# First norm's sums from the feature-major input, the residual loaded later, features in 4 KB rows, the second chunk parted in halves

## The chip, the cores and the metric

The kernel runs on one core of a Trainium2 chip. The metric is the device time of one execution in microseconds; lower is better.

## What is computed

A segment of a decoder trunk on 256 tokens of width 2048, in f32: a recurrent layer (HGRN2) and then a differential-attention layer, each with an MLP and a gated embedding behind it. Only the beginning matters here: a norm over the features, and the projections that read it.

```
def rms_norm(x, gain):
    xf = x.astype(jnp.float32)
    y = xf * lax.rsqrt(jnp.mean(xf * xf, axis=-1, keepdims=True) + EPS)
    return (y * gain.astype(jnp.float32)).astype(x.dtype)
...
        h = rms_norm(x, ln_mix[i])
        if i < N_A:
            proj = h @ a_w_in[j]
            q_a, f_a, in_a, g_a = (t.reshape(b, s, A_HEADS, A_HEAD_DIM) for t in jnp.split(proj, 4, axis=-1))
            f = lb + (1.0 - lb) * jax.nn.sigmoid(f_a.astype(jnp.float32))
            o = hgrn2_chunkwise(jax.nn.silu(q_a), 1.0 - f, in_a, jnp.log(f))
            ...
            x = x + o.reshape(b, s, A_WIDTH).astype(x.dtype) @ a_w_out[j]
```

## The kernel before

All weights are read once, in chunks of 256 rows by 512 columns (512 KB each; `raw`, four buffers). A matrix product in nearly full f32 is made of parts: ACT rounds a chunk to a short format (`hi`, a cast), DVE subtracts that from the chunk (`lo`), and PE multiplies hi and lo with the activations, which are parted in the same way. hi and lo have three buffers each. A group is 512 output columns, eight chunks. In the groups used at the start (`group_b`: queries and forget gates, tokens as columns) each chunk gives PE eight pairs of matmuls, one hi 128x512 and one lo 128x256, into two PSUM tiles.

The gain of a norm is applied to its input ahead of the product (`gained`: one ACT instruction and one DVE instruction for each 128 features, here `gain_xa`), and the factor of each token, 1/sqrt(mean square), only to the result. So the first projection can start on x before its norm is known. x comes twice: `x_t` (features in partitions, 16 blocks of 128x256) into `xa`, two blocks a load, and `x_r` (tokens in partitions) into `x`, the residual, 512 columns a load. The first group is number 4, the first forget gates; group 0, the first queries, follows. `do_f` and `do_q` put the results through `project`, whose `evac` adds the halves of a PSUM tile and multiplies by the factor of the token, `RR[0]` (a row, the same in all partitions; `RR[1]` holds it with tokens in partitions).

Work that runs beside the chunks is written as generators (`gens`); `pump()` takes one step of each behind every chunk. `start()` is such a generator: per step it loads the next two blocks of `xa`, applies the gain, from the fifth step on loads a quarter of `x` and lets ACT square and sum it (`Norm.square`), and at the end DVE adds the sums, ACT takes the root (`rsqrt`: Ln and Exp), and a matmul of ones with a diagonal spreads the factors over all partitions. The compiler's scheduler then orders each engine's instructions; every engine runs its own in that order. All loads leave SP's queue in the order that it shows.

`accd` and the masks are POOL's only work; `lambdas()` and `bounds()` are small computations from the table `sml`. `x` is first used as the residual long after the start, where the layer's output is added. The chunks of a group are counted from 0 here, and "chunk 7" is the last one of group 4 where no group is named.

Of the kernel before, what the change touches and what calls it, by code (L numbers as in the profile page):

```python
# [17 lines left out]
P = 128  # L18
T = 256
# [20 lines left out]
def kernel(ctx: ExitStack, tc: tile.TileContext, a):  # L40
# [54 lines left out]
    def chunk(src):  # L95
        raw = rp.tile([P, KCS, CW], F32, tag="raw", name="raw")
        nc.sync.dma_start(raw.rearrange("p a b -> p (a b)"), src)
        hi = wp.tile([P, KCS, CW], F32R, tag="hi", name="hi")
        lo = wp.tile([P, KCS, CW], F32R, tag="lo", name="lo")
        nc.scalar.copy(hi, raw)  # L100
        nc.vector.tensor_tensor(lo, raw, hi.bitcast(F32), ALU.subtract)  # L101
        return hi, lo
# [48 lines left out]
    def group_b(wsrc, g, rhs, evac, pump=None, fresh=0, by_part=False):  # L151

        ps = [mm.tile([P, 2, CW], F32, tag="mm", name="mmps") for _ in range(2)]
        w = []
        for c in range(NCH):
            w.append((chunk if c or not fresh else first_chunk)(wsrc[g, c]))
            if c < fresh:
                mm_first(ps, *w[c], rhs, c)  # L160
            else:
                mm_b(ps[0], *w[c], rhs, 0, c * KCS, c == 0, c == NCH - 1, by_part and c == 0)
                for d in ([c] if fresh or c > 1 else [0, 1] if c else []):
                    mm_b(ps[1], *w[d], rhs, 1, d * KCS, d == 0, d == NCH - 1)
            if pump:
                pump()
        for pair in range(2):
            evac(4 * (g % 4) + 2 * pair, ps[pair])
# [36 lines left out]
    class Norm:  # L205
        def __init__(self, outs=(), row=False):
            self.outs, self.row = outs, row
# [27 lines left out]
        def finish(self, box):  # L235
# [4 lines left out]
            if self.row:  # L240
                dg = ev.tile([P, T], F32, tag="rr", name="dg", bufs=1)
                for tt in range(2):
                    nc.vector.tensor_scalar(dg[:, tt * P:(tt + 1) * P], ident, rc[:, tt, 0:1], None, ALU.mult)
                ps = sm.tile([P, 512], F32, tag="sm", name="smps")
                nc.tensor.matmul(ps[:, :T], ones, dg, start=True, stop=True)
                r = ev.tile([P, T], F32, tag="rn", name="rn", bufs=2)
                nc.scalar.copy(r, ps[:, :T])
            else:
                r = ev.tile([P, 2, 1], F32, tag="r2", name="r2", bufs=2)
                nc.vector.tensor_tensor(r, rc, rc, ALU.mult)  # L250
# [72 lines left out]
    nrm = Norm(row=True)  # L323
# [7 lines left out]
    def load_xa(c):  # L331
        nc.sync.dma_start(xa[:, 2 * c:2 * c + 2], a["x_t"][:, 2 * c:2 * c + 2])
# [45 lines left out]

    def start():

        for c in range(8):
            if c < 7:
                load_xa(c + 1)
                gain_xa(c + 1)
            if c == 3:
                nc.sync.dma_start(sml, a["small"])
                nc.sync.dma_start(ident, a["ident"])
            if c == 6:
                bounds()
            if c > 3:  # L390
                g = c - 4
                nc.sync.dma_start(x[:, :, g * CW:(g + 1) * CW], a["x_r"][:, :, g * CW:(g + 1) * CW])
                nrm.square(g)
            if c < 7:
                yield
        yield from nrm.finish(RR)
        for _ in range(4):
            yield
        for b in range(2):
# [3 lines left out]
        lambdas()  # L403

# [3 lines left out]
    with hs:  # L408
# [134 lines left out]
        def project(g):  # L543
# [3 lines left out]
            def evac(m, ps):  # L547
# [5 lines left out]
                nc.vector.tensor_tensor(t, lo, t, ALU.add)  # L553
                nc.vector.tensor_tensor(o, t, bc(RR[0], 2).rearrange("p m (c t) -> p m c t", c=2), ALU.mult)
# [4 lines left out]
        def do_f(j):  # L559
            s = st[j]  # L560
            z = project(4 + j)
# [369 lines left out]
```

## Time and profile before

| | us |
|---|---|
| median of 3 runs (lowest, highest) | 2508.78 (2508.29, 2509.92) |
| the profiled execution | 2508.73 |
| its span in the trace | 2506.9 |
| PE busy | 2497.7 |
| DVE busy | 1544.4 |
| ACT busy | 1301.8 |
| POOL busy | 7.1 |

The span runs from the first to the last instruction of the trace; the execution's own time holds some 2 us around it. PE is busy nearly all the time by the profile, so its idle stretches are few, and they are found in the waits of PE, in the chain of waits that ended last, and by reading the timeline. "PEld" is the load of weights into PE, which runs beside the matmuls. An f32 matmul is two instructions in the profile where its operands are not of the rounded kind.

### The profile page before, as it was taken

Reading aid. Unit: us, or ns where it says so; the run is one execution under the profiler, and the core shown is the slowest. Engines: PE = TensorE matmul, PEld = TensorE weight load, DVE = VectorE, ACT = ScalarE, POOL = GpSimd, SP = SyncE. Lnnn points to the kernel's source line nnn. Section 1 sums busy time; section 2 is a strip of 40 time slices with the busy share of each in tenths; the row PEclk is TensorE's granted clock in tenths of the full one; section 3 lists DMA queues with packets and bytes.
Section 4 is the critical chain, followed back from the end, with each engine's and each line's share of the span. In section 5 each row is a group of like instructions: output and inputs, shape, how many; then the busy total and the mean of one; then the engine's idle time right before and its main releaser. Section 6 shows DMA issues by size and latency. Waiting matters only on the chain.

```text
span 2506.9 us, 32220 instructions
## 1 busy us (share of the span) xinstructions
PE 2497.7 (100%) x12546; PEld 2113.1 (84%) x12546; DVE 1544.4 (62%) x1755; ACT 1301.8 (52%) x1659; POOL 7.1 (0%) x12
## 2 busy tenths in 40 slices
PE   9999999999999999999999999999999999999999
PEld 8888888888888888888888888888888888888887
DVE  7887886555565465565575576556555556555555
ACT  8666665544344444444576565544434434444455
POOL 0000000000000000000000000000000000000000
PEclk9999999999999999999999999999999999999999
DMA  7545455555555555565555545555556555555555
GB/s 274 181 152 180 160 169 180 185 188 191 193 190 195 193 187 193 193 192 186 187 180 188 185 151 173 167 184 187 193 187 194 192 193 190 196 190 189 189 188 168
DMA packets 130377, 466.99 MB, mean 186 GB/s; under 512 B 14512, under 2 KB 14896, under 8 KB 130224
## 3 DMA queue, kind: packets, MB, share of 16 engines
q1 hardware_dynamic: 130080, 464.93, 56.3%
q8 instruction: 98, 1.61, 0.3%
q14 instruction: 55, 0.45, 0.1%
q10 hardware_dynamic: 144, 0.01, 0.0%
HBM read 462.78 MB, written 2.10 MB: 185 GB/s over the span
## 4 chain that ended last, share of the span: by engine, by line
PE 96%; DVE 2%; ACT 1%; DMA 1%; issue 1%; SPq 0%; DVEq 0%; ACTq 0%
PE mmps L145 23%; PE mmps L178 19%; PE mmps L176 19%; PE mmps L177 19%; PE mmps L148 11%; PE smps L225 1%; PE smps L487 1%; DVE lo L101 1%; DMA x<-x_r 0%; PE smps L754 0%; PE smps L817 0%; PE smps L789 0%; DMA raw<-w_in 0%; ACT hi L100 0%; PE smps L518 0%
## 5 line engine op out<-in xcount | busy, mean ns | idle before, releaser
L101 DVE TENSOR_TENSOR lo<-raw,hi 128x1024 fp32r<-128x1024 f32 x871 | 1065.2, 1224 | 877.9 <-ACT hi L100 877.2
L100 ACT CAST hi<-raw 128x1024 fp32r<-128x1024 f32 x871 | 914.8, 1051 | 1052.8 <-PE mmps L178 618.8
L145 PE MATMUL mmps<-big,hi 128*128 128x512 f32 x2544 | 885.9, 394 | 0.0
L176 PE MATMUL mmps<-hi,big 128*128 128x512 f32 x2176 | 853.8, 392 | 0.0
L178 PE MATMUL mmps<-hi,big 128*128 128x512 f32 x2176 | 848.2, 390 | 0.0
L177 PE MATMUL mmps<-lo,big 128*128 128x512 f32 x2176 | 848.1, 390 | 0.0
L148 PE MATMUL mmps<-big,lo 128*128 128x256 f32 x2544 | 704.3, 278 | 0.3 <-DVE lo L101 0.3
L145 PEld LDWEIGHTS mmps<-big,hi 128*128 128x128 f32 x2544 | 476.3, 188 | 108.4
L178 PEld LDWEIGHTS mmps<-hi,big 128*128 128x128 f32 x2176 | 408.5, 188 | 85.9 <-DVE big L123 0.3
L148 PEld LDWEIGHTS mmps<-big,lo 128*128 128x128 f32 x2544 | 478.3, 188 | 2.8 <-DVE lo L101 0.9
L177 PEld LDWEIGHTS mmps<-lo,big 128*128 128x128 f32 x2176 | 408.8, 188 | 82.4
L176 PEld LDWEIGHTS mmps<-hi,big 128*128 128x128 f32 x2176 | 408.7, 188 | 82.1
L303 DVE SCALAR_TENSOR_TENSOR x<-mmps,r,x 128x512 f32<-128x512 f32 x64 | 45.1, 747 | 13.1 <-PE mmps L178 13.1
L201 ACT ACTIVATE big<-smps,sml 128x256 fp32r<-128x256 f32 x96 | 41.1, 471 | 18.1 <-DVE big L202 18.1
L123 DVE TENSOR_TENSOR big<-u,big 128x512 fp32r<-128x512 f32 x72 | 49.4, 686 | 0.0
L202 DVE SCALAR_TENSOR_TENSOR big<-smps,sml,big 128x256 fp32r<-128x256 f32 x96 | 42.3, 479 | 6.8 <-ACT big L201 6.5
L636 DVE SCALAR_TENSOR_TENSOR u<-u 128x512 f32<-128x512 f32 x64 | 44.3, 692 | 2.2
L122 ACT CAST big<-u 128x512 fp32r<-128x512 f32 x72 | 44.4, 616 | 1.9 <-DVE u L636 1.9
L294 ACT COPY t<-mmps 128x512 f32<-128x512 f32 x64 | 37.3, 583 | 14.5 <-PE mmps L148 14.5
L295 DVE TENSOR_TENSOR u<-mmps,t 128x512 f32<-128x512 f32 x64 | 43.8, 684 | 0.0
L213 ACT ACTIVATE t<-x 128x512 f32<-128x512 f32 x48 | 30.2, 630 | 3.8 <-DVE x L666 2.5
L487 PEld LDWEIGHTS smps<-B,A 128*128 128x128 f32 x160 | 20.0, 191 | 2.7 <-DVE on L528 1.1
(193 smaller groups left out, 892.8 us busy)
## 6 DMA issues: line engine op xcount, KB each, us to landing
raw<-w_up SPq DMA_DIRECT2D x256, 512.0 KB, 3.9
raw<-w_dn SPq DMA_DIRECT2D x256, 512.0 KB, 3.3
raw<-w_in SPq DMA_DIRECT2D x127, 512.0 KB, 3.3
raw<-w_pg SPq DMA_DIRECT2D x64, 512.0 KB, 3.3
raw<-w_ao SPq DMA_DIRECT2D x32, 512.0 KB, 3.3
raw<-w_k SPq DMA_DIRECT2D x32, 512.0 KB, 3.7
raw<-w_q SPq DMA_DIRECT2D x32, 512.0 KB, 3.9
raw<-w_v SPq DMA_DIRECT2D x32, 512.0 KB, 3.3
```

The source lines that it names most:

```text
L100: nc.scalar.copy(hi, raw)
L101: nc.vector.tensor_tensor(lo, raw, hi.bitcast(F32), ALU.subtract)
L122: nc.scalar.copy(dst[:, k, 0, :], src)
L123: nc.vector.tensor_tensor(dst[:, k, 1, :], src, dst[:, k, 0, :].bitcast(F32), ALU.subtract)
L145: nc.tensor.matmul(ps[:, ml, :], hi[:, k, w:w + P], rhs[:, k0 + k].rearrange("p a t -> p (a t)"), start=first and k == 0, stop=False)
L148: nc.tensor.matmul(ps[:, ml, T:2 * T], lo[:, k, w:w + P], rhs[:, k0 + k, 0, :], start=False, stop=last and k == KCS - 1)
L176: nc.tensor.matmul(out, xs[:, kc0 + k, 0, ts], hi[:, k], start=st, stop=False)
L177: nc.tensor.matmul(out, xs[:, kc0 + k, 0, ts], lo[:, k], start=False, stop=False)
L178: nc.tensor.matmul(out, xs[:, kc0 + k, 1, ts], hi[:, k], start=False, stop=en)
L303: nc.vector.scalar_tensor_tensor(xg, ps[:, tt], scale[:, tt, 0:1], xg, ALU.mult, ALU.add)
L487: nc.tensor.matmul(ps[:, i], A[:, i], B[:, :, i], start=True, stop=True)
L636: nc.vector.scalar_tensor_tensor(u, u, 0.0, u, ALU.max, ALU.mult)
```

## The change

The sums of squares of the first norm are made from `xa` instead of `x`: ACT squares two blocks at a time, POOL adds up the squares (the sum sits in a corner of `x`, which is not loaded yet), DVE adds its two halves, and three f32 matmuls with ones add over the partitions: one 128x256 that gives the sums as a row in all partitions, and two of one column that give them with tokens in partitions. ACT takes the root of all 258 columns at once. The residual `x` is loaded in two loads of 1 MB (8 KB rows), some dozen chunks later. `xa` comes in loads of four blocks from the third on. The identity is loaded behind the first group. The second chunk's hi and lo are made in two halves. In the first group the product with the token's factor is taken out of `evac` and stands in a generator of its own, `first_keys`, in front of what follows from it (`keys`).

```diff
@@ -92,13 +92,14 @@
         return ap[:, None, :].broadcast_to([P, n, ap.shape[-1]])
 
 
-    def chunk(src):
+    def chunk(src, apart=False):
         raw = rp.tile([P, KCS, CW], F32, tag="raw", name="raw")
         nc.sync.dma_start(raw.rearrange("p a b -> p (a b)"), src)
         hi = wp.tile([P, KCS, CW], F32R, tag="hi", name="hi")
         lo = wp.tile([P, KCS, CW], F32R, tag="lo", name="lo")
-        nc.scalar.copy(hi, raw)
-        nc.vector.tensor_tensor(lo, raw, hi.bitcast(F32), ALU.subtract)
+        for k in (slice(0, 1), slice(1, 2)) if apart else (slice(0, 2),):
+            nc.scalar.copy(hi[:, k], raw[:, k])
+            nc.vector.tensor_tensor(lo[:, k], raw[:, k], hi[:, k].bitcast(F32), ALU.subtract)
         return hi, lo
 
     def first_chunk(src):
@@ -155,7 +156,7 @@
         ps = [mm.tile([P, 2, CW], F32, tag="mm", name="mmps") for _ in range(2)]
         w = []
         for c in range(NCH):
-            w.append((chunk if c or not fresh else first_chunk)(wsrc[g, c]))
+            w.append(chunk(wsrc[g, c], c < fresh) if c or not fresh else first_chunk(wsrc[g, c]))
             if c < fresh:
                 mm_first(ps, *w[c], rhs, c)
             else:
@@ -203,8 +204,8 @@
 
 
     class Norm:
-        def __init__(self, outs=(), row=False):
-            self.outs, self.row = outs, row
+        def __init__(self, outs):
+            self.outs = outs
             self.ss = ev.tile([P, 2, 4], F32, tag="ss", name="ss", bufs=2)
 
         def square(self, g):
@@ -237,17 +238,8 @@
             rc = ev.tile([P, 2, 1], F32, tag="rc", name="rc", bufs=2)
             nc.vector.tensor_reduce(rc, self.ss, axis=AX.X, op=ALU.add)
             rsqrt(rc, rc, 1.0 / D)
-            if self.row:
-                dg = ev.tile([P, T], F32, tag="rr", name="dg", bufs=1)
-                for tt in range(2):
-                    nc.vector.tensor_scalar(dg[:, tt * P:(tt + 1) * P], ident, rc[:, tt, 0:1], None, ALU.mult)
-                ps = sm.tile([P, 512], F32, tag="sm", name="smps")
-                nc.tensor.matmul(ps[:, :T], ones, dg, start=True, stop=True)
-                r = ev.tile([P, T], F32, tag="rn", name="rn", bufs=2)
-                nc.scalar.copy(r, ps[:, :T])
-            else:
-                r = ev.tile([P, 2, 1], F32, tag="r2", name="r2", bufs=2)
-                nc.vector.tensor_tensor(r, rc, rc, ALU.mult)
+            r = ev.tile([P, 2, 1], F32, tag="r2", name="r2", bufs=2)
+            nc.vector.tensor_tensor(r, rc, rc, ALU.mult)
             box.extend((r, rc))
             yield
 
@@ -320,7 +312,6 @@
     hg = hs.enter_context(pool("hg", 2, "left"))
     xa = s2.tile([P, KC, T], F32, tag="big", name="xa")
     xs = moving(s1)
-    nrm = Norm(row=True)
     RR = []
 
 
@@ -328,8 +319,9 @@
     for _ in range(11):
         nc.tensor.matmul(wps[:, 0:P], ones, ones, start=True, stop=True)
 
-    def load_xa(c):
-        nc.sync.dma_start(xa[:, 2 * c:2 * c + 2], a["x_t"][:, 2 * c:2 * c + 2])
+    def load_xa(c, n=1):
+        m = slice(2 * c, 2 * (c + n))
+        nc.sync.dma_start(xa[:, m], a["x_t"][:, m])
 
     def gain_xa(c):
         for m in (2 * c, 2 * c + 1):
@@ -376,31 +368,56 @@
         nc.vector.tensor_scalar(nlam, nlam, -LAM_INIT, None, ALU.add)
         nc.vector.tensor_scalar(gsub, sml[:, C_SUB:C_SUB + 2], 1.0 - LAM_INIT, None, ALU.mult)
 
+
+    acc = x[:, 0, 0:CW].rearrange("p (a t) -> p a t", a=2)
+
+    def square_xa(c):
+        o = ev.tile([P, 2, T], F32, tag="t", name="t") if c else acc
+        nc.scalar.activation(o, xa[:, 2 * c:2 * c + 2], AF.Square)
+        if c:
+            nc.gpsimd.tensor_tensor(acc, acc, o, ALU.add)
+
+    def first_norm():
+
+        nc.vector.tensor_tensor(acc[:, 0], acc[:, 0], acc[:, 1], ALU.add)
+        yield
+        ps = sm.tile([P, 512], F32, tag="sm", name="smps")
+        nc.tensor.matmul(ps[:, :T], ones, acc[:, 0], start=True, stop=True)
+        for tt in range(2):
+            nc.tensor.matmul(ps[:, T + tt:T + tt + 1], acc[:, 0, tt * P:(tt + 1) * P], ones[:, 0:1], start=True, stop=True)
+        r = ev.tile([P, T + 2], F32, tag="rn", name="rn", bufs=1)
+        rsqrt(r, ps[:, :T + 2], 1.0 / D)
+        RR.extend((r[:, 0:T], r[:, T:T + 2].rearrange("p (t o) -> p t o", o=1)))
+
     def start():
 
         for c in range(8):
+            if c == 0:
+                load_xa(1)
+            elif c in (1, 3, 5):
+                load_xa(c + 1, 2)
             if c < 7:
-                load_xa(c + 1)
                 gain_xa(c + 1)
-            if c == 3:
+            square_xa(c)
+            if c == 4:
                 nc.sync.dma_start(sml, a["small"])
-                nc.sync.dma_start(ident, a["ident"])
             if c == 6:
                 bounds()
-            if c > 3:
-                g = c - 4
-                nc.sync.dma_start(x[:, :, g * CW:(g + 1) * CW], a["x_r"][:, :, g * CW:(g + 1) * CW])
-                nrm.square(g)
             if c < 7:
                 yield
-        yield from nrm.finish(RR)
-        for _ in range(4):
-            yield
+        yield from first_norm()
+        for _ in range(3):
+            yield
+        nc.sync.dma_start(ident, a["ident"])
         for b in range(2):
             load_mask(b)
             yield
         nc.sync.dma_start(cmask, a["cmask"])
         lambdas()
+        for tt in range(2):
+            for _ in range(4):
+                yield
+            nc.sync.dma_start(x[:, tt], a["x_r"][:, tt])
 
     gens.append(start())
 
@@ -540,7 +557,7 @@
                 nc.vector.scalar_tensor_tensor(O[:, m, 1, :], ps, gain, O[:, m, 0, :].bitcast(F32), ALU.mult, ALU.subtract)
                 yield
 
-        def project(g):
+        def project(g, scaled=True):
 
             z = hg.tile(H4, F32, tag="z", name="z", bufs=1)
 
@@ -550,15 +567,29 @@
                 t = ev.tile([P, 2, T], F32, tag="t", name="t")
                 nc.scalar.copy(t, ps[:, :, T:2 * T])
                 t, lo = (u.rearrange("p m (c t) -> p m c t", c=2) for u in (t, ps[:, :, 0:T]))
-                nc.vector.tensor_tensor(t, lo, t, ALU.add)
-                nc.vector.tensor_tensor(o, t, bc(RR[0], 2).rearrange("p m (c t) -> p m c t", c=2), ALU.mult)
+                nc.vector.tensor_tensor(t if scaled else o, lo, t, ALU.add)
+                if scaled:
+                    nc.vector.tensor_tensor(o, t, bc(RR[0], 2).rearrange("p m (c t) -> p m c t", c=2), ALU.mult)
 
             group_b(a["w_in"], g, xs, evac, pump, fresh=2 if g == 4 else 0)
             return z
 
         def do_f(j):
+            z = project(4 + j, j > 0)
+            if j:
+                keys(j, z)
+            else:
+                gens.append(first_keys(z))
+
+        def first_keys(z):
+
+            for c in range(2):
+                nc.vector.tensor_tensor(z[:, c], z[:, c], bc(RR[0][:, c * P:(c + 1) * P], 4), ALU.mult)
+            keys(0, z)
+            yield
+
+        def keys(j, z):
             s = st[j]
-            z = project(4 + j)
             k = s["k"] = hg.tile(H4, F32, tag="k", name="k")
             G = s["G"] = hg.tile(H4, F32, tag="G", name="G")
             sigmoid(k, z, G)
```

ACT, from the first hi cast on. Of before (`raw_129` is chunk 0, `raw_164` chunk 1, `raw_191` chunk 2, `raw_218` chunk 3, `raw_247` chunk 4; `big_103` is the input with its gain, `x2` two instructions in a row):

```order
L114 CAST hi_130<-raw_129 128x512
L201 ACTIVATE big_103<-xa_102,gain0_84 128x256 x2
L114 CAST hi_130<-raw_129 128x512
L201 ACTIVATE big_103<-xa_102,gain0_84 128x256 x2
L100 CAST hi_166<-raw_164 128x1024
L201 ACTIVATE big_103<-xa_102,gain0_84 128x256 x2
L100 CAST hi_193<-raw_191 128x1024
L201 ACTIVATE big_103<-xa_102,gain0_84 128x256 x2
L100 CAST hi_220<-raw_218 128x1024
L201 ACTIVATE big_103<-xa_102,gain0_84 128x256 x2
L100 CAST hi_249<-raw_247 128x1024
L201 ACTIVATE big_103<-xa_102,gain0_84 128x256 x2
```

Of after (`raw_128`, `raw_164`, `raw_196` and `raw_225` are chunks 0 to 3; `x_98` holds the running sum, `t_193`, `t_222`, `t_252` the squares of xa 1 to 3):

```order
L115 CAST hi_129<-raw_128 128x512
L376 ACTIVATE x_98<-xa_102 128x512
L202 ACTIVATE big_103<-xa_102,gain0_84 128x256 x2
L115 CAST hi_129<-raw_128 128x512
L202 ACTIVATE big_103<-xa_102,gain0_84 128x256 x2
L376 ACTIVATE t_193<-xa_102 128x512
L101 CAST hi_166<-raw_164 128x512 x2
L202 ACTIVATE big_103<-xa_102,gain0_84 128x256 x4
L101 CAST hi_198<-raw_196 128x1024
L376 ACTIVATE t_222<-xa_102 128x512
L376 ACTIVATE t_252<-xa_102 128x512
L101 CAST hi_227<-raw_225 128x1024
```

A square now stands ahead of the first gains, chunk 1's cast is in two, and between chunk 1's cast and that of chunk 2 there are four gains where there were two; two squares stand ahead of chunk 3's cast. Before, the first squares stood ahead of the cast of chunk 5.

DVE, where the first group ends. Of before (`raw_350` is chunk 7, `raw_421` the first chunk of group 0, `raw_435` the second; L238 reduces the sums):

```order
L101 TENSOR_TENSOR lo_312<-raw_309,hi_311 128x1024
L202 SCALAR_TENSOR_TENSOR big_103<-xa_102,gain0_84,big_103 128x256 x2
L101 TENSOR_TENSOR lo_353<-raw_350,hi_352 128x1024
L238 TENSOR_REDUCE rc_376<-ss_104 128x2
L101 TENSOR_TENSOR lo_424<-raw_421,hi_423 128x1024
L243 TENSOR_SCALAR dg_380<-ident_96,rc_376 128x128 x2
L553 TENSOR_TENSOR t_387<-mmps_127,t_387 128x512
L553 TENSOR_TENSOR t_391<-mmps_128,t_391 128x512
L101 TENSOR_TENSOR lo_438<-raw_435,hi_437 128x1024
L554 TENSOR_TENSOR z_126<-t_387,rn_385 128x2x2x128
L554 TENSOR_TENSOR z_126<-t_391,rn_385 128x2x2x128
```

Of after (`raw_315` is chunk 6, `raw_354` chunk 7, `raw_389` and `raw_435` the first two of group 0; L382 is the add of the sum's halves, which needs POOL's last add):

```order
L102 TENSOR_TENSOR lo_318<-raw_315,hi_317 128x1024
L351 TENSOR_TENSOR lb_119<-lbe_117,lbs_118 128x16
L352 TENSOR_SCALAR lb_119<-lb_119 128x16
L353 TENSOR_SCALAR omlb_120<-lb_119 128x16
L382 TENSOR_TENSOR x_98<-x_98 128x256
L102 TENSOR_TENSOR lo_357<-raw_354,hi_356 128x1024
L102 TENSOR_TENSOR lo_392<-raw_389,hi_391 128x1024
L102 TENSOR_TENSOR lo_438<-raw_435,hi_437 128x1024
L570 TENSOR_TENSOR z_125<-mmps_126,t_380 128x2x2x128
L102 TENSOR_TENSOR lo_468<-raw_465,hi_467 128x1024
L570 TENSOR_TENSOR z_125<-mmps_127,t_383 128x2x2x128
L587 TENSOR_TENSOR z_125<-z_125,rn_407 128x512 x2
```

The add of the sums stands ahead of chunk 7's lo; before, the reduction of the sums stood behind it. The product by the factor (L554, now L587) still stands behind both adds of the PSUM halves (L553, now L570), but one chunk of group 0 further back.

POOL, the whole of its work up to the masks. Of before:

```order
L71 MEMSET segm_92 128x256
L426 MEMSET accd_644 128x1024
L72 MEMSET segm_92 128x4
L426 MEMSET accd_1109 128x1024
L341 CAST masks_95<-mf_531 128x512
```

Of after:

```order
L72 MEMSET segm_92 128x4
L443 MEMSET accd_1112 128x1024
L378 ISA
L378 TENSOR_TENSOR x_98<-x_98,t_193 128x512
L378 TENSOR_TENSOR x_98<-x_98,t_222 128x512
L378 TENSOR_TENSOR x_98<-x_98,t_252 128x512
L378 TENSOR_TENSOR x_98<-x_98,t_281 128x512
L378 TENSOR_TENSOR x_98<-x_98,t_312 128x512
L378 TENSOR_TENSOR x_98<-x_98,t_341 128x512
L378 TENSOR_TENSOR x_98<-x_98,t_376 128x512
```

An instruction listed as ISA and seven adds stand between the clearing of `accd` and the masks; each add reads a tile of squares that ACT writes, and there are two such tiles in turn.

## Rows read from the trace of the kernel before

**Rows 1.** The page: its head, and PE busy: us (share of the span), instructions.

```profile
span 2506.9 us, 32220 instructions
...
PE 2497.7 (100%) x12546; PEld 2113.1 (84%) x12546; DVE 1544.4 (62%) x1755; ACT 1301.8 (52%) x1659; POOL 7.1 (0%) x12
```

**Rows 2.** Waits of PE, whole run: waited for, us in total, times, longest.

```profile
PE mmps L133 <- ACT hi L100: 0.7, 1, 0.7
...
PE mmps L148 <- DVE lo L101: 0.3, 1, 0.3
```

**Rows 3.** The chain that ended last, in order of time: start us, us, what.

```profile
15.19 9.11 DMA x<-x_r
...
26.78 1.24 DVE lo L101
```

**Rows 4.** Timeline, 0 to 9 us: start us, us, engine line operation [idle <-releaser].

```profile
4.39 0.69 DVE L115 TENSOR_TENSOR lo<-raw,hi 128x512 fp32r<-128x512 f32 x1 [2.38 <-ACT hi L114]
...
5.06 0.91 ACT L201 ACTIVATE big<-xa,gain 128x256 fp32r<-128x256 f32 x2 [0.70 <-DMA xa<-x_t]
...
5.60 0.89 DVE L202 SCALAR_TENSOR_TENSOR big<-xa,gain,big 128x256 fp32r<-128x256 f32 x2 [0.52 <-ACT big L201]
5.87 0.60 ACT L114 CAST hi<-raw 128x512 fp32r<-128x512 f32 x1
...
6.14 1.19 PE L133 MATMUL mmps<-big,hi 128*128 128x512 f32 x4 [0.91 <-DVE big L202]
...
7.57 0.91 ACT L201 ACTIVATE big<-xa,gain 128x256 fp32r<-128x256 f32 x2 [1.09 <-DMA xa<-x_t]
...
8.81 1.04 ACT L100 CAST hi<-raw 128x1024 fp32r<-128x1024 f32 x1 [0.33 <-DMA raw<-w_in]
```

**Rows 5.** The same, 9 to 31 us.

```profile
9.88 1.23 DVE L101 TENSOR_TENSOR lo<-raw,hi 128x1024 fp32r<-128x1024 f32 x1 [0.89 <-ACT hi L100]
...
15.94 0.39 PE L145 MATMUL mmps<-big,hi 128*128 128x512 f32 x1
...
17.04 0.23 ACT L355 ACTIVATE lbe<-lbe 128x48 f32<-128x48 f32 x1
...
17.21 0.63 ACT L213 ACTIVATE t<-x 128x512 f32<-128x512 f32 x1
...
18.02 0.39 PE L145 MATMUL mmps<-big,hi 128*128 128x512 f32 x1
...
18.29 0.17 DVE L356 TENSOR_TENSOR lbs<-lbe 128x16 f32<-128x16 f32 x1
...
28.06 0.38 PE L148 MATMUL mmps<-big,lo 128*128 128x256 f32 x1 [0.30 <-DVE lo L101]
...
30.49 0.39 PE L145 MATMUL mmps<-big,hi 128*128 128x512 f32 x1
```

**Rows 6.** One window: busy PE, PEld, DVE, ACT, POOL, granted clock, DMA share, GB/s.

```profile
10.00:20.00 10.00, 9.94 (x56) 8.37 (x57) 9.71 (x24) 9.08 (x19) 0.00 (x0) 1.00 1.05 397
```

**Rows 7.** Timeline of PE around the matmul for lambda.

```profile
50.33 0.27 PE L148 MATMUL mmps<-big,lo 128*128 128x256 f32 x1
...
50.58 0.48 PE L145 MATMUL mmps<-big,hi 128*128 128x512 f32 x1
50.90 0.28 PE L148 MATMUL mmps<-big,lo 128*128 128x256 f32 x1
```

**Rows 8.** Timeline of POOL, and of DVE beside it.

```profile
1.91 1.00 POOL L426 MEMSET accd<- 128x1024 f32 x1
34.68 1.69 POOL L341 CAST masks<-mf 128x512 uint8<-128x512 f32 x1 [31.77 <-DMA mf<-masks]
37.44 1.09 POOL L341 CAST masks<-mf 128x512 uint8<-128x512 f32 x1 [1.06 <-DMA mf<-masks]
...
34.69 1.22 DVE L101 TENSOR_TENSOR lo<-raw,hi 128x1024 fp32r<-128x1024 f32 x1
```

**Rows 9.** DMA issues, 0 to 60 us: count, KB each, median us to landing.

```profile
x<-x_r SPq DMA_DIRECT2D x4, 512.0 KB, 8.1
```

## The prediction

> **What bounds it now.** I read the page first: PE is busy for 2497.7 of 2506.9 us [rows 1], so only what PE waits for, or what is put on it, can move the end. Then the waits of PE over the whole run: the long ones are few, and those of the matmuls at the start stand among them [rows 2]. The change touches the first group of projections (group 4, the forget gate: 64 pairs of matmuls, one with hi and one with lo) and what lies just behind it, so the rest is read from the timeline of the first 35 us.
>
> Two numbers frame that stretch. The first real matmul starts at 6.14 us [rows 4], the first of the next group at 30.49 us [rows 5]: 24.35 us. Six pairs take 18.02 - 15.94 = 2.08 us [rows 5], so a pair takes 0.347 us, a chunk of eight pairs 2.78 us and the group 22.2 us if nothing is late. The start loses 2.1 us to late operands. The chain of waits says to what: from 15.19 us it runs through the load of x, then through the lo of the last chunk [rows 3], and the matmul that was late for that lo is the one at 28.06 us [rows 5]. In the same stretch the DMA queues move 397 GB/s with every engine taken (share 1.05) [rows 6].
>
> So at most 2.1 us of gaps and the 6.14 us before the first matmul are there to be had. The four loads that come first stand in the same order before and after, so the 6.14 us don't shrink. A measurement of this kernel tells about 0.2% (5.0 us) from no change: a gain of that size has no source here.
>
> **The loads.** Before chunk 7's weights, three loads of x (512 KB each) and the identity leave SP's queue; of xa's eight loads the first two stay, and the other six become three with rows of 4 KB. By the rate of 397 GB/s a weight chunk or a doubled xa load takes 1.3 us. What lands first is as before: xa 0 at 5.06, xa 1 at 7.57, chunk 1 at 8.81 us, by the ACT instructions that waited for them [rows 4]. From there, in SP's new order: xa 2 and 3 at 10.1, chunk 2 at 11.4, chunk 3 at 12.8, xa 4 and 5 at 14.1, chunk 4 at 15.4, chunk 5 with the small table at 17.0, xa 6 and 7 at 18.3, chunk 6 at 19.6, chunk 7 at 20.9 us. The last is some 4.8 us before ACT took it in the old kernel (its hi ends as lo starts, at 26.78 us [rows 3]). The wait for x is gone. What is late next is ACT's own queue, in which the squares now stand.
>
> **ACT's queue, after.** Durations: square 0.63, two gains 0.91, a hi 1.04, half a hi 0.60 [rows 4, 5]. The square of xa 0 stands ahead of xa 0's gains: 5.06 to 5.69, gains to 6.60, second half hi to 7.20. Gains of xa 1 from 7.57 to 8.48, square 9.11, the two halves of chunk 1 at 9.71 and 10.31, four gains 12.13, hi of chunk 2 13.17. Two squares, hi 3 at 15.47, four gains, hi 4 at 18.33, two squares, hi 5 at 20.63, the exponential of the bounds 0.23 [rows 5], four gains, hi 6 at 23.72, two squares to 24.98, hi 7 at 26.02. ACT never rests from 7.57 on; that is the new bound.
>
> **DVE's queue, after.** A lo takes 1.23, half a lo 0.69, two gain products 0.89, a small operation 0.17 [rows 4, 5]. Halves of chunk 1 end at 10.45 and 11.14, four products at 12.95, lo 2 from 13.20 to 14.43, lo 3 at 16.73, four products and a small one, lo 4 at 19.91, four small ones, lo 5 at 21.9, four products, three small ones, lo 6 at 25.4, three small ones 25.9. Then comes the one new wait of DVE: the last add of the sums, which needs POOL's seventh add. Behind it stand lo 7 and all later lo. POOL's add (128x512, two inputs) is in no row. Its nearest rows are POOL's cast of as many elements, 1.09 us alone and 1.69 us beside DVE [rows 8]; the kind without input, 1.00 us for twice the elements, is farther [rows 8]. I take 1.09 and keep 1.69: the last two adds run from 24.35 to 26.53 (or 27.73), DVE's add to 26.98 (28.2; at most 0.45, as a product), lo 7 to 28.2 (29.4).
>
> **PE, after.** The first matmul came 1.08 us after ACT's first gain (5.06 to 6.14 [rows 4]); the square moves that to 6.77. First chunk to 9.55. The parted chunk 1 is there at 9.76 by halves, and its sixteen matmuls end at 12.54, against 13.1 before. Chunk 2 is the step that gives this back: its first two hi matmuls run, then PE waits for the lo of 14.43 (hop 0.06), and the other 2.32 us end at 16.81. Chunk 3 ends at 19.59, chunk 4 waits 0.15 for its lo, 22.5, chunk 5 25.3, chunk 6 28.1, chunk 7 has its lo at 28.27 where it needs it at 28.3. End of the group: 30.9 us, 0.4 later than 30.49. With the slow add it would be 32.0.
>
> **The two single-column matmuls.** The f32 matmul of the row sums costs what that with the diagonal cost (128x256 both). Two of one column are added. Such a one stands in the trace, the 128x2 for lambda: from one lo matmul to the next it is 50.90 - 50.33 = 0.57 us in place of 0.347 [rows 7], so 0.22 us each and 0.44 us in all. They wait for DVE's add (26.98), long done when PE comes to them.
>
> **What costs nothing, and its cover.** The norm's two activations and the delayed products: the sums' matmuls follow four pairs of group 0 (30.9 + 1.4 = 32.3 us) and end near 33.4 (0.6 for the wide one, an estimate from the wide matmul's columns). Ln and Exp of 258 columns lie between 0.23 (48 columns) and 0.63 (512 columns), so 0.8 for both; two products of half a lo's kind 1.4; then stand on ACT the first step of the sigmoid and the hi of group 0's chunk 3, 1.04 each, and on DVE its lo, 1.23 [rows 4, 5]: 38.9 us. PE has twenty pairs until then (chunk 1 with the second half of chunk 0, and chunk 2), 6.9 us, and needs that lo at 40.7. If those 1.8 us of cover were gone, each us would cost one. The residual: two loads of 1 MB (2.6 us each at the rate above) go out behind the weights of chunks 6 of group 0 and 0 of the next, and wait for the sums to be read. Four weight tiles are ahead of PE there, 11 us; a load took 8.1 us to land in the worst stretch of the old start [rows 9]. Norm's reduction and the two products with the identity (DVE) and the copy of the row (ACT) go, all behind the group's last lo, where PE had cover already. Order on all engines is unchanged past some 60 us, so nothing later moves by itself.
>
> **Sum.** The profiled execution took 2508.73 us, 1.8 us more than its span and within 0.05 of the median 2508.78. 2508.73 + 0.4 + 0.44 = 2509.6 us.
>
> **Rivals.**
> POOL's first add late. Ahead of the adds POOL's program has a new instruction listed as ISA, which reloads the library of POOL's routines, and no row of before shows one. POOL reaches it at 2.91 us (1.91 + 1.00 [rows 8]). The first add's data are there at 9.11, but ACT's square of xa 3 reuses that buffer at 13.81: with 1.09 for the add, a reload up to 9.8 us costs nothing. Beyond, the square waits, and the hi of chunks 3 to 7 stand behind it on ACT, so that each us costs PE about one. The nearest row to such a fetch is the slowest landing of a load, 8.1 us [rows 9]; I take it as no longer than that, which is nothing on the path. Two in a row, 16.2 us, I take as the other end: the reload is done at 19.1 us, PE begins to lose from 13.0 on, and 6.1 us give 2515.7 us. It is slower by 0.2% from about 14 us of reload on. This is the case on the other side. I give it 0.12. The Trainium skill (GPSIMD Engine Reference, Instruction dispatch) has about 6 us for the first call of a freshly loaded routine; by that the reload is done before 9.11 and the sum stays; no row here shows it.
>
> POOL and DVE shut each other out. If an add kept DVE's two-input operations waiting for its whole 1.09 us, seven would take 7.6 us from a queue that is idle for about 4.0 us of its 23.8 from 4.39 us on (19.8 us of work by the durations above): 3.6 us more, 2513.2 us; with 1.69 it is 7.8 us and 2517.4. From 1.17 us an add on it passes the 0.2%. Against it: the cast at 34.68 us ran beside a lo that began at 34.69, and the lo took 1.22 us, as ever; POOL took 0.60 us longer [rows 8]. I give it 0.14, 0.03 of that beyond 0.2%. This is a rule of the Trainium skill (SBUF — State Buffer, Who interferes with whom): whoever starts first holds the shared port for the whole instruction and the other fully blocks. The rows agree only in part, since POOL lost half of the lo's time and DVE nothing.
>
> ACT isn't the bound. If its instructions overlap a little and chunk 2's lo is there in time, PE runs from 6.77 with the 0.2 us wait for chunk 1 alone: the group ends at 29.2, 1.3 earlier, and 0.44 for the two matmuls goes against it: 2507.9 us. For it speaks that the rows on ACT start up to 0.1 us before the one ahead ends [rows 4]; against it that lo 2 would have to come 1.6 us sooner. 0.15.
>
> **Chances.** Forecast 0.57 (2508.5 to 2511.0, with the slow add in it), ACT free 0.15, the port 0.14, the late add 0.12; a gain of 5 us by something unseen 0.02. Faster 0.02, slower 0.12 + 0.03 = 0.15, same 0.83. The range leaves out the late add, the upper end of the port and the unseen gain: 2507.3 to 2513.3 us.
>
> **What would show it.** First matmul at 6.8 us, because a square stands ahead of the first gains. PE waits for DVE's lo at chunk 2, near 13.7 to 14.5, and hardly at chunk 7. No wait for x in the chain. POOL's first add ends before 13.8 us; the seventh near 26.5, with DVE's add right behind. The next group begins near 30.9 us. I am wrong if the first add starts after some 13 us, if DVE's lo beside POOL's adds take over 1.3 us, or if the next group begins before 30 us.

## The result, and the profile after

The changed kernel takes 2513.28 us (median of 20 runs, 2511.38 to 2515.47), the kernel before 2509.02 us beside it (20 runs). The ratio is 1.0016, 95% interval 1.001 to 1.0022: 4.3 us slower, within the 0.2% that the prediction calls no change, and at the upper edge of its range (2507.3 to 2513.3). The profiled execution took 2513.73 us, 5.0 more than that of before, and its span is 5.0 longer too. The interval lies above 1, so the change does cost time.

The page and the waits of PE in the first 60 us (waited for, us in total, times, longest); they answer [rows 1, 2]:

```profile
span 2511.9 us, 32224 instructions
...
PE 2501.5 (100%) x12550; PEld 2116.0 (84%) x12550; DVE 1549.7 (62%) x1754; ACT 1300.4 (52%) x1651; POOL 16.7 (1%) x19
```

```profile
PE mmps L149 <- DVE lo L102: 3.1, 2, 2.6
...
PE mmps L134 <- ACT hi L101: 0.5, 1, 0.5
```

PE waits twice for a lo of DVE; the shorter of the two (0.5 us) was forecast, the one of 2.6 us was not. The chain of waits (start, us, what) leads to it, where [rows 3] led through the load of x:

```profile
10.32 1.71 ACT big L202 x4
...
17.84 3.33 DVE big L203 x3
21.26 1.14 DVE lo L102
22.45 0.39 PE mmps L149
```

The load is gone from the chain, as forecast. In its place stand three of DVE's gain products, 1.1 us each, where two in a row take 0.89 [rows 4]. The timeline of PE and ACT at the same places as [rows 4, 5]:

```profile
4.52 0.63 ACT L376 ACTIVATE x<-xa 128x512 f32<-128x512 f32 x1
...
6.12 1.20 PE L134 MATMUL mmps<-big,hi 128*128 128x512 f32 x4
...
14.29 0.39 PE L149 MATMUL mmps<-big,lo 128*128 128x256 f32 x1 [0.53 <-DVE lo L102]
...
22.45 0.39 PE L149 MATMUL mmps<-big,lo 128*128 128x256 f32 x1 [2.56 <-DVE lo L102]
...
23.05 0.63 PE L146 MATMUL mmps<-big,hi 128*128 128x512 f32 x1
...
26.25 0.45 PE L146 MATMUL mmps<-big,hi 128*128 128x512 f32 x1
...
35.14 0.40 PE L146 MATMUL mmps<-big,hi 128*128 128x512 f32 x1
...
36.44 0.28 PE L149 MATMUL mmps<-big,lo 128*128 128x256 f32 x1
36.55 0.59 PE L385 MATMUL smps<-x,ones 128*128 128x256 f32 x2
36.98 0.50 PE L387 MATMUL smps<-ones,x 128*128 128x1 f32 x4
...
37.67 0.28 PE L149 MATMUL mmps<-big,lo 128*128 128x256 f32 x1
```

The two lo matmuls of the kernel before, ahead of its matmul for the sums and behind it:

```profile
31.15 0.28 PE L148 MATMUL mmps<-big,lo 128*128 128x256 f32 x1
...
31.93 0.28 PE L148 MATMUL mmps<-big,lo 128*128 128x256 f32 x1
```

The first matmul starts as before (6.12 us, before 6.14). The next group starts at 35.14 us, before at 30.49: 4.65 us, nearly the whole loss. The rest are the two single-column matmuls: from the lo matmul ahead of the sums to the one behind there are 1.23 us (36.44 to 37.67) where there were 0.78 (31.15 to 31.93), so 0.45 us. 4.65 + 0.45 = 5.1, against 5.0 by the spans.

And what followed the wait, by windows (columns as in [rows 6]; the granted clock is the third number from the end):

```profile
20.00:22.40 2.40, 0.00 (x0) 0.00 (x0) 2.40 (x4) 0.00 (x0) 0.89 (x1) 1.00 0.03 14
22.40:26.30 3.90, 3.85 (x14) 3.34 (x15) 3.83 (x13) 3.53 (x8) 0.08 (x1) 0.57 0.65 180
26.30:36.00 9.70, 9.70 (x56) 8.44 (x56) 7.84 (x9) 4.82 (x6) 3.28 (x2) 1.00 0.59 188
```

PE rested for 2.56 us, and when it went on, the granted clock was 0.57 of full in the stretch to 26.3 us, mostly the lower of its two levels (1.2 and 2.4 GHz). Five pairs there, from 23.05 to 26.25 us, take 0.64 us each in place of 0.347: 1.5 us lost. So 2.56 + 1.5 = 4.1 of the 4.65 us lie at this one place.

POOL and DVE at that place, each addition as a record of its own (windows cut between them), the place of [rows 8]:

```profile
13.65 1.74 POOL L378 TENSOR_TENSOR x<-x,t 128x512 f32<-128x512 f32 x1 [3.43 <-ACT t L376]
15.47 2.17 POOL L378 TENSOR_TENSOR x<-x,t 128x512 f32<-128x512 f32 x1
18.19 1.30 POOL L378 TENSOR_TENSOR x<-x,t 128x512 f32<-128x512 f32 x1 [0.55 <-ACT t L376]
19.57 1.32 POOL L378 TENSOR_TENSOR x<-x,t 128x512 f32<-128x512 f32 x1
...
14.99 1.48 DVE L102 TENSOR_TENSOR lo<-raw,hi 128x1024 fp32r<-128x1024 f32 x1 [0.76 <-ACT hi L101]
16.39 1.52 DVE L203 SCALAR_TENSOR_TENSOR big<-xa,gain,big 128x256 fp32r<-128x256 f32 x1
...
18.24 2.93 DVE L203 SCALAR_TENSOR_TENSOR big<-xa,gain,big 128x256 fp32r<-128x256 f32 x2
```

Add the durations to the starts. The first product ends at 17.91, 0.27 us behind the end of the addition at 15.47 (17.64); the last two end at 21.17, 0.28 behind the end of the addition at 19.57 (20.89). The four products take 4.78 us; four that stand alone take 1.67 (E1 below). Each side waits for the end of what the other has begun. Chunk 4's lo, which comes next in DVE's order but for one small operation, therefore starts only at 21.18 us, and that is what PE waits for.

### The profile page after: what moved, and what is told of

Same layout as the page of the kernel before. It is cut to its first block, busy times and chain, and to the rows that moved or that the text cites. A ratio compares the mean times of both kernels' runs of the same rounds, so it can differ in the third digit from the quotient of the medians.

```text
span 2511.9 us, 32224 instructions
## 1 busy us (share of the span) xinstructions
PE 2501.5 (100%) x12550; PEld 2116.0 (84%) x12550; DVE 1549.7 (62%) x1754; ACT 1300.4 (52%) x1651; POOL 16.7 (1%) x19
## 4 chain that ended last, share of the span: by engine, by line
PE 96%; DVE 2%; ACT 1%; issue 1%; DMA 0%; SPq 0%; DVEq 0%
PE mmps L146 23%; PE mmps L179 19%; PE mmps L177 19%; PE mmps L178 19%; PE mmps L149 12%; PE smps L226 1%; PE smps L504 1%; DVE lo L102 0%; DMA xa<-x_t 0%; PE smps L785 0%; PE smps L848 0%; PE smps L820 0%; ACT hi L101 0%; PE smps L535 0%; PE smps L467 0%
## 5 line engine op out<-in xcount | busy, mean ns | idle before, releaser
L102 DVE TENSOR_TENSOR lo<-raw,hi 128x1024 fp32r<-128x1024 f32 (+1 forms) x872 | 1065.4, 1223 | 878.5 <-ACT hi L101 877.9
L101 ACT CAST hi<-raw 128x1024 fp32r<-128x1024 f32 (+1 forms) x872 | 914.8, 1049 | 1056.2 <-PE mmps L179 618.9
L214 ACT ACTIVATE t<-x 128x512 f32<-128x512 f32 x40 | 25.1, 629 | 3.3 <-DVE x L697 2.5
```

The costliest lines, as they stand in the source:

```text
L101: nc.scalar.copy(hi[:, k], raw[:, k])
L102: nc.vector.tensor_tensor(lo[:, k], raw[:, k], hi[:, k].bitcast(F32), ALU.subtract)
```

## The experiments

**E1: no additions on POOL.** Two lines (`if c: nc.gpsimd.tensor_tensor(acc, acc, o, ALU.add)`) are gone.

> The changed kernel without POOL's seven adds; the sums hold the first two blocks only, so what the adds compute is left out. Theory 1 (POOL's adds and DVE's two-input operations exclude each other): the four gain products that took 4.78 us take 1.7 us again, chunk 4's lo ends near 19.4 us where PE needs it at 19.9, no stall there and no stretch at a granted clock under 1.0; the group behind the first begins near 30.6 us instead of 35.1, the time is 0.5 us over the kernel before (0.45 us of that the two single-column matmuls): ratio 1.0002. Theory 2 (the squares crowd ACT's queue, POOL is a bystander): the squares are still there, the next group begins after 33 us, ratio 1.001 or more.

Measured: 2508.64 us, ratio 0.9999 (0.999 to 1.0008). DVE in its timeline:

```profile
15.69 1.67 DVE L203 SCALAR_TENSOR_TENSOR big<-xa,gain,big 128x256 fp32r<-128x256 f32 x4
...
17.83 1.22 DVE L102 TENSOR_TENSOR lo<-raw,hi 128x1024 fp32r<-128x1024 f32 x1
```

The products are back at 1.67, chunk 4's lo starts 3.35 us sooner (21.18 before), the granted clock is 1.00 from 10 to 36 us, and the next group begins at 30.67 us where 30.6 was expected. The whole loss hangs on the additions. It also prices them: against this run the changed kernel's DVE lost 0.38 us at the halves of chunk 1, 0.25 at lo 3, 3.11 at the four products, and 1.09 and 0.97 at two small operations beside the last two additions: 5.8 us together. (The matmuls of the sums move to the front in this kernel, since they have nothing to wait for.)

**E2: the additions on DVE.**

```
-            nc.gpsimd.tensor_tensor(acc, acc, o, ALU.add)
+            nc.vector.tensor_tensor(acc, acc, o, ALU.add)
```

> The changed kernel with the seven adds on DVE instead of POOL. Theory 1: nothing is shut out any more, but DVE gets seven adds of about 0.7 us (4.9 us in all) where it had some 4 us idle: PE waits for some lo by 1 to 2 us in all, in pieces, the next group begins at 31 to 32.5 us, ratio 1.0004 to 1.0010. Theory 2 (ACT's queue): 35 us as with POOL, ratio 1.0016.

Measured: 2509.24 us, ratio 1.0002 (0.9992 to 1.0011). One addition and the lo behind it:

```profile
19.04 0.69 DVE L378 TENSOR_TENSOR x<-x,t 128x512 f32<-128x512 f32 x1
19.64 1.22 DVE L102 TENSOR_TENSOR lo<-raw,hi 128x1024 fp32r<-128x1024 f32 x1
```

The same seven additions take 0.69 us each on the engine they were to relieve, 4.8 us in all: less than the 5.8 that it lost by their being on POOL. In the first 60 us no wait of PE for an operand of the group but the 0.53 at chunk 2 is left, and the next group begins at 30.50 us. The expectation was too dark: it had PE wait for 1 to 2 us more and the group begin at 31 to 32.5. ACT's squares are all there in this run, so they are not the cause.

**E3: clears in place of the additions.** Three memsets of the tile of squares for each addition, so that POOL waits for and runs beside the same things, but reads nothing.

> The changed kernel with each POOL add replaced by three POOL clears of the tile of squares (about 1.5 us of POOL work that waits for the square in the same way, holds the tile in the same way, but reads nothing from SBUF); the sums are left out. If an add shuts DVE out because it reads SBUF: DVE's four products take 1.7 us, as without adds, next group near 30.6 us, ratio 1.0002. If any POOL instruction shuts DVE out, or the wait of ACT's squares for POOL is the cause: products stretched or squares late, next group at 33 us or later, ratio 1.001 or more.

Measured: 2508.67 us, ratio 0.9999 (0.999 to 1.0009). POOL's clears and DVE's products:

```profile
14.10 3.32 POOL L379 MEMSET t<- 128x512 f32 x6 [3.22 <-ACT t L376]
...
16.15 1.67 DVE L203 SCALAR_TENSOR_TENSOR big<-xa,gain,big 128x256 fp32r<-128x256 f32 x4
```

Products run at 1.67 us beside clears, and the lo that runs beside them (15.01 us) takes 1.23, so neither POOL's being busy nor its waits are the cause; its reading is. (One small operation with one input, L352, is an exception: its record is 1.24 us long beside the clears, 0.18 in E1. The lo behind it took 1.23 as ever.)

**E5: PE kept busy in its rest.** Ten matmuls into a tile that nothing reads, ahead of chunk 4's.

```
+            if fresh and c == 4:
+                keep = sm.tile([P, 512], F32, tag="sm", name="keep")
+                for _ in range(10):
+                    nc.tensor.matmul(keep, w[4][0][:, 0, 0:P], ..., start=True, stop=True)
```

> The changed kernel with ten more matmuls (hi of chunk 4 with older features, 128x512, into a PSUM tile that nobody reads; 2.3 us of PE work) ahead of chunk 4's, where PE waits 2.56 us for the lo. If the granted clock of 0.57 in 22.4 to 26.3 us comes from PE's rest before it: the wait for the lo ends at the same 22.4 us, but PE goes on at clock 1.0, a pair takes 0.35 instead of 0.64 us, the next group begins near 33.5 us instead of 35.1, and the time is 1.6 us under the changed kernel: ratio to the kernel before about 1.0010. If the drop has another cause, the pairs after 22.4 us stay at 0.64 us and the ratio stays 1.0016 or rises.

Measured: 2512.51 us, ratio 1.0015 (1.0005 to 1.0024); the times alone don't separate it from the changed kernel, the trace does. Windows and PE:

```profile
22.40:26.30 3.90, 3.83 (x22) 3.42 (x23) 3.83 (x14) 3.51 (x8) 0.05 (x1) 1.00 0.59 190
```

```profile
22.47 0.38 PE L149 MATMUL mmps<-big,lo 128*128 128x256 f32 x1 [0.30 <-DVE lo L102]
...
31.35 0.39 PE L149 MATMUL mmps<-big,lo 128*128 128x256 f32 x1 [0.29 <-DVE lo L102]
35.40 0.59 PE L389 MATMUL smps<-x,ones 128*128 128x256 f32 x2
```

Chunk 4's lo comes at the same time, but the clock stays at 1.00, and the next group begins at 34.01 us in place of 35.14 (33.5 expected). The sums' matmul comes at 35.40 in place of 36.55: 1.15 us sooner, and 0.29 are lost to a new wait for chunk 7's lo (31.35 us), which stands behind DVE's add that needs POOL's last one. Together 1.44, the 1.5 of the clock. The fall of the clock is thus the rest's doing, and what PE loses by the late lo itself remains.

**E8: every addition twice.**

```
-            nc.gpsimd.tensor_tensor(acc, acc, o, ALU.add)
+            for _ in range(2):
+                nc.gpsimd.tensor_tensor(acc, acc, o, ALU.add)
```

> The changed kernel with every add of a square on POOL done twice: fourteen adds where there were seven (the sum is therefore not the one wanted). Theory, the adds shut out DVE's two-input operations: about as much again is lost as the seven took, 4 to 8 us on top of the changed kernel's 2513.3, so 2517 to 2521, with DVE's gain products and lo stretched at more places than in the changed kernel. Rival, the adds only cost through the last one, which DVE's add of the halves waits for: the queue of POOL grows by seven adds of 1.3 us, the last ends some 3 us later at most, 2515 to 2516, and DVE's operations ahead of it keep the durations of the changed kernel.

Measured: 2519.28 us, ratio 1.0043 (1.0029 to 1.0057): 6.0 us on top of the changed kernel, inside what the theory gave and outside the rival's.

```profile
15.05 4.50 DVE L102 TENSOR_TENSOR lo<-raw,hi 128x1024 fp32r<-128x1024 f32 x2
...
19.48 5.77 DVE L203 SCALAR_TENSOR_TENSOR big<-xa,gain,big 128x256 fp32r<-128x256 f32 x4
```

```profile
17.39 0.58 PE L149 MATMUL mmps<-big,lo 128*128 128x256 f32 x1 [3.61 <-DVE lo L102]
...
27.60 0.39 PE L149 MATMUL mmps<-big,lo 128*128 128x256 f32 x1 [1.84 <-DVE lo L102]
...
40.17 0.39 PE L149 MATMUL mmps<-big,lo 128*128 128x256 f32 x1 [1.07 <-DVE lo L102]
```

The two lo take 2.25 us each on average, a product 1.44, and PE waits 6.5 us in three places. The last of them (1.07 us) is the rival's: it is for the lo behind DVE's add of the halves, which waited 2.56 us for POOL's last addition. The other 5.4 us are not.

**E9 and E10: a copy, or a cast to 8 bits, in place of the addition.** One input is read in place of two; the second has the form of the cast on which the prediction rested.

```
-            nc.gpsimd.tensor_tensor(acc, acc, o, ALU.add)
+            nc.gpsimd.tensor_copy(acc, o)
```

> The changed kernel with each add on POOL replaced by a copy of the new squares into the sum's place (128x512 f32, one input read instead of two; the sum is left out). Waits and order stay. Theory A, any read of SBUF by POOL shuts DVE's two-input operations out: the four gain products near 16 us still take over 2.5 us (4.78 with the adds, 1.7 without), a lo beside a copy over 1.5 us, and 1 to 4 us of the 4.3 are left, 2510 to 2513. Theory B, only an operation with two inputs does: the products take 1.7 and the lo 1.23 us, no fall of PE's clock, 2508.5 to 2509.5.

> The changed kernel with each add on POOL replaced by a cast of the new squares to 8 bits (128x512 uint8 from f32, the form of the cast on which the prediction rested; the sum is left out). Waits and order stay. Theory A, the cast shuts DVE out like an add, and the one row of before (lo beside a cast: 1.22 us) only shows a lo that had begun with it or ahead of it: the gain products take over 2.5 us, 2510 to 2513. Theory B, a cast leaves DVE alone, whenever it starts: products 1.7 us, lo 1.23, casts of 1.1 to 1.7 us, 2508.5 to 2509.5.

Measured: 2509.35 us, ratio 0.9998 (0.9989 to 1.0007), and 2509.49 us, ratio 0.9998 (0.9989 to 1.0008); the kernel before took 2510.32 us beside them. By the times, theory B; by the records, neither as it was put. Of E9, POOL and DVE:

```profile
17.87 2.35 POOL L378 COPY x<-t 128x512 f32<-128x512 f32 x2 [2.79 <-ACT t L376]
...
17.74 1.22 DVE L102 TENSOR_TENSOR lo<-raw,hi 128x1024 fp32r<-128x1024 f32 x1
18.88 0.60 DVE L345 TENSOR_TENSOR lbm<-lbm,sml 128x16 f32<-128x16 f32 x1
...
19.66 1.63 DVE L102 TENSOR_TENSOR lo<-raw,hi 128x1024 fp32r<-128x1024 f32 x1
```

The lo at 17.74 began ahead of the copy and took its usual 1.22; the small operation behind it took 0.60 in place of 0.17 and the next lo 1.63. E10 has the same figures to 0.02 us. So a copy and a cast shut out as well. What differs is how long each is. Where DVE does nothing beside it (from 35.93 to 38.00 us in E10), the cast of the masks takes 0.61 us:

```profile
36.22 0.61 POOL L333 CAST masks<-mf 128x512 uint8<-128x512 f32 x1 [1.43 <-DMA mf<-masks]
```

At 0.61 us DVE loses 0.2 to 0.4 at a time, POOL is done before DVE comes to its products at 16.07 us (1.66 us long), and DVE's slack covers the rest. At 1.3 it does not. No product ran beside a copy or a cast in these two runs; that those shut out is read from the lo and the small operation.

**E6 and E7: the other parts, each alone on the kernel before.** E6 has only the two halves of chunk 1 (`apart=c < fresh`), E7 only the larger loads of xa (`load_xa(c + 1, 2)` in three steps).

> The kernel before with the second chunk's hi and lo in two halves and nothing else. Theory: PE's wait for the second chunk's hi (0.7 us in the kernel before) falls to about 0.2, and the half us is mostly lost again at a later chunk, as ACT and DVE have two instructions more (0.16 us each): the next group begins at 30.0 to 30.6, 2508.3 to 2509.0. Rival, the halves cost more than they give, since lo of chunk 2 comes later: up to 0.4 us more, 2509.3.

> The kernel before with the feature-major input in rows of 4 KB (six of its eight loads become three) and nothing else. Theory: the total to be loaded ahead of chunk 7 is the same, so the last lo comes as late, and only the order changes: xa 2 and 3 together ahead of chunk 2 cost that chunk up to 0.6 us of landing, for which PE waits, 2508.7 to 2509.3. Rival, larger rows move faster: the window of 10 to 20 us shows over 410 GB/s (397 before), and the next group begins 0.5 to 1 us sooner, 2507.8 to 2508.3.

Measured: E6 2508.61 us, ratio 1.0 (0.9991 to 1.0009); E7 2509.06 us, ratio 1.0001 (0.9992 to 1.001). E6's waits of PE:

```profile
13.27 0.39 PE L149 MATMUL mmps<-big,lo 128*128 128x256 f32 x1 [0.49 <-DVE lo L102]
...
24.94 0.39 PE L149 MATMUL mmps<-big,lo 128*128 128x256 f32 x1 [0.20 <-DVE lo L102]
...
28.28 0.38 PE L149 MATMUL mmps<-big,lo 128*128 128x256 f32 x1 [0.27 <-DVE lo L102]
```

The wait for chunk 1's hi (0.7 in [rows 2]) is gone, and 0.49 at chunk 2 and 0.20 at chunk 6 have taken its place. E7's profile has PE's longer wait at chunk 1 and a fall of the clock behind it:

```profile
10.39 1.19 PE L133 MATMUL mmps<-big,hi 128*128 128x512 f32 x4 [1.67 <-ACT hi L100]
```

```profile
13.00:16.00 3.00, 3.00 (x11) 2.53 (x10) 2.93 (x5) 2.78 (x6) 0.00 (x0) 0.55 1.04 395
```

The loads up to chunk 1 stand in the same order as before, so that wait (1.67 us, 0.7 before) isn't the order's doing; why chunk 1 landed later in this execution stays open. In E10, with the same order again, ACT's wait for chunk 1 ended later still (9.46 us; 9.29 in E7, 8.81 before). The profiled execution of E7 was one of its longer ones (2510.10 us, where its runs go from 2507.73 to 2510.39). Its window of 10 to 20 us moved 402 GB/s (397 before): larger rows move no faster to speak of.

**E4: the residual moved behind the first group, in the kernel before.** With it go the identity and the norm, and the product with the token's factor waits in a generator as in the changed kernel; the cut shows the loads.

```
-            if c > 3:
-                g = c - 4
-                nc.sync.dma_start(x[:, :, g * CW:(g + 1) * CW], ...)
-                nrm.square(g)
...
+        for g in range(5):
+            if g < 4:
+                nc.sync.dma_start(x[:, :, g * CW:(g + 1) * CW], ...)
+            if g:
+                nrm.square(g - 1)
+            yield
         yield from nrm.finish(RR)
```

> The kernel before with one thing moved: the loads of the residual, their squares on ACT and the norm come behind the first group instead of beside its second half, and the product with the token's factor in the first group waits in a generator as in the changed kernel. No square of the input, no work for POOL, no halves, no larger loads. Theory, what the start of the kernel before lost (the wait for x in the chain, then for the lo of the last chunk, 0.30 us for PE at 28.06) came from the residual's loads in the group: they are gone, the next group begins 0.3 to 1.5 us sooner than 30.49, and the time is 2507.3 to 2508.6 (0.07 to 0.01 per cent less than before). Rival, the loads are as late behind the first group, and group 0's chunks pay what group 4 has gained: 2508.5 to 2510, no difference.

Measured: 2509.05 us, ratio 1.0002 (0.9993 to 1.0011). The wait has moved into the next group, as the rival had it:

```profile
36.35 0.38 PE L148 MATMUL mmps<-big,lo 128*128 128x256 f32 x1 [0.31 <-DVE lo L101]
```

Before, it stood at 28.06 us with 0.30 [rows 5]. The next group did begin sooner in the profiled execution, as the theory had it: at 29.30 us in place of 30.49, 0.71 of these 1.19 us because the first matmul came at 5.43. The rest of the run gives it back, for the span is 2506.8 us (2506.9 before). Taking the residual out of the first group, which is what the change is built around, gives nothing that can be measured by itself.

## Why the prediction was right, and where it was wrong

The bound that it set on a gain held: there were 2.1 us of gaps to be had, and E2 and E4, which take the loads out without POOL, measure no difference. "Within 0.2%" held too, but not by the likeliest case. What happened is its second rival, POOL and DVE shutting each other out, to which it gave 0.14 and 2513.2 us. One of its own signs of being wrong came true, too: a lo of DVE beside POOL's adds took 1.48 us, over the 1.3 that it had set.

**The step that failed** is the argument against that rival: "the cast at 34.68 us ran beside a lo that began at 34.69, and the lo took 1.22 us, as ever; POOL took 0.60 us longer". The lo had the first turn, and the cast waited for it, though its record starts 0.01 us earlier: DVE was still in the two-input product by the token's factor, which stands ahead of the lo and ends at 34.77. The cast ends at 34.68 + 1.69 = 36.37, 0.46 us behind the end of the lo (34.69 + 1.22 = 35.91). The second cast of [rows 8], which the prediction called alone, has this lo of the kernel before beside it:

```profile
36.83 1.23 DVE L101 TENSOR_TENSOR lo<-raw,hi 128x1024 fp32r<-128x1024 f32 x1 [0.93 <-ACT hi L100]
```

That lo ends at 38.06, the cast at 38.53, 0.47 behind it. Both casts ran behind a lo, not beside one or alone, and 1.09 us was no price: the same cast takes 0.61 us where DVE leaves it alone. Two starts close together and one undisturbed duration show who came first, not that nobody waits; the ends show it. The rule that the prediction set beside the row, the Trainium skill (SBUF — State Buffer, Who interferes with whom: the one that starts first has the shared port for its whole instruction, and the other waits), agrees with the pairs of products, lo, additions and casts shown here, in that one runs whole and the other ends behind it; which of two was first can't be read from starts 0.01 us apart. The same section's remark that DVE's operations with two inputs meet only those of POOL that read agrees with E3.

**The price of an add.** Taken at 1.09, kept to 1.69; measured 1.28 to 1.32 where it did not wait (1.74, 2.05 and 2.17 where it did), above the 1.17 from which the rival was to pass 0.2%. With 1.3 the rival's own sum would have been 7 x 1.3 - 4.0 = 5.1 us on top of 2509.6, so 2514.7 us, outside the range. The rival had seven adds block DVE for 7.6 us less 4.0 of slack. By E1 DVE lost 5.8 us, of which 3.7 lay ahead of chunk 4's lo; that lo came 2.56 us late for PE; and 1.5 us of lower clock came on top, of which no step of the prediction spoke. So the rival had the mechanism right and its terms wrong, and that its 2513.2 us lies next to the measured 2513.28, which is 0.02 us inside the range, is luck. So is that the loss stopped at 0.17%.

**ACT as the bound.** It held up to chunk 2, where the forecast wait came (0.53 us, at 14.29 for a forecast 14.49). From chunk 4 on DVE was the bound: between 20 and 22.4 us ACT does nothing (0.00 in the window shown), while DVE's products wait.

**The first matmul** was to come at 6.77, since a square stood ahead of the gains. It came at 6.12: xa 0 was there by 4.52 us, when ACT's first cast had ended, not at 5.06 as in [rows 4]. In E9 ACT's wait for it ended at 4.35. The landing of the first load differs by 0.7 us between executions, and the step took one of them for fixed.

**The last add of the sums** was to be at 26.5 us; the seventh addition on POOL ended at 29.66, and DVE's add came at 29.70. Lo 7 behind it was still in time, because PE was late already; E5, where PE was sooner, paid 0.29 us for it.

**What held by its numbers:** two single-column matmuls 0.45 us (forecast 0.44); the norm's chain and the residual's loads in the second stretch, for which PE waits nowhere in the first 60 us; the reload of POOL's library (MODIFY_POOL_CONFIG, issued at 2.9 us), since the first addition starts at 8.95, right behind its square (8.25 + 0.62 = 8.87), so the case of 2515.7 us fell.

## What to carry to other kernels

An addition of two inputs on POOL did not run beside DVE's own two-input work here; each waited for the other's instruction to end. So before moving such work to POOL, count its duration there against DVE's slack (here 0.69 us on DVE against 1.3 on POOL, and E2 was the better place). To see from a trace whether two engines shut each other out, compare ends, not starts: an operation that waited ends behind the other by a time that was the same for its kind here (a product 0.27 to 0.28 us, a cast 0.46 to 0.47, a lo 1.07 to 1.08). And where one engine is busy nearly all the time, a gain is bounded by its gaps in that stretch; look for that bound first, since a change that can only gain 0.1% can still lose more.

## What the runs showed that was not expected

- DVE's products end 0.27 to 0.28 us behind the end of an add of POOL, POOL's casts 0.46 to 0.47 behind the end of a lo, and a lo that waited 1.07 to 1.08 behind the end of an add (changed kernel, 14.99 us), a copy or a cast (E9, E10): instructions take turns. For products and lo this holds only where POOL reads; clears on POOL left the products at 1.67 us and a lo at 1.23.
- Small operations were held, too, some with one input: L353 took 1.14 us beside the seventh add, 0.17 in E1, and L352 1.24 us beside clears. Why a one-input operation is held by a clear was not tested.
- Of the 4.1 us that a stall cost, 1.5 came after it: PE rested for 2.56 us, and the granted clock was 0.57 in the next 3.9 us; with filler matmuls in the rest it was 1.00 (E5). In E7 a rest of 1.67 us was followed by 0.55 from 13 to 16 us; in E4 one of 0.89 us was followed by none.
- The first load landed 0.7 us apart in executions of kernels that issue it alike (ACT started on it at 5.06 in the kernel before, at 4.35 in E9).
